# The opening of a transformer step: u's first products by one channel tile at a time, other queues for the small loads, weights asked for two chunks ahead

## The chip, the cores and the metric

The kernel runs on one core of a Trainium2 chip. It is one program, launched once. The metric is the device time of one execution in microseconds: 1690.18 in the median of three runs (1689.3 to 1690.31). The core has five engines with queues of their own: TensorE (PE, with its weight loads as PEld), VectorE (DVE), ScalarE (ACT), GpSimd (POOL) and SyncE (SP), which here only issues transfers.

## The reference, cut to what matters

One layer (D = 2048, 128 context tokens and 256 latent ones, so 384 token rows) does a token mixing and then an MLP. Only its beginning is touched by the change: the modulation's scale and shift, the normalised and modulated input h, and the first part of the projection h @ w_in.

```python
def _adaln(cond, ada_w, ada_b):
    mod = jax.nn.silu(cond) @ ada_w + ada_b
    return mod.reshape(cond.shape[0], N_MOD, D_MODEL)
...
    h = _rmsnorm(x, norm_w[0]) * (1 + scale_a) + shift_a
    proj = h @ w_in
    q, k, v, o, g, u = jnp.split(proj, [M, 2 * M, 3 * M, 4 * M, 4 * M + N_GATES * N_HEADS], axis=-1)
```

The context rows are modulated by c_ctx, the latent rows by c. u (1024 columns) feeds a pooling mixer, v and the gates g feed a bidirectional mLSTM; q, k, the output projection and the MLP come later.

## The kernel before

All products are in float32, split in two: an operand is a rounded part (hi) and the rest (lo), and a product takes three matmuls, hi by hi, lo of the input by hi of the weight, hi of the input by lo of the weight. ACT writes hi (L134 for weights, L447 for h), DVE writes lo (L135, L448). load_w loads a weight chunk through one of three raw buffers and splits it into one of N_W = 4 hi and 4 lo buffers.

The projection's u, v and gates are summed over the 16 channel tiles of 128 in eight steps of two tiles (ksteps). In each step h is formed for the two tiles by make_h, and five chunks of columns take their products (chunk list at L434): u 0 to 511, u 512 to 1023, and v in 384, 384 and 256 plus 32 gate columns. The sums of a chunk lie in three banks of the pool psum, one for each 128 token rows; the pool has eight banks of 128 x 512 floats, and everything that PE writes takes one of them. At a chunk's end the banks are copied to u_sb or vsb (first step, ACT, L514) or added there (later steps, DVE, L516).

h needs the scale (part 1 of ada_w) and the shift (part 0) of its channels. first_ada forms them for the two tiles of each step, as a generator that is advanced at places written out by hand: each next() issues a load of a slab of ada_w (512 KB: 128 partitions by 1024 floats) and its matmuls (L256), then copies the sum to SBUF (ada_sb, L268), and at last adds it up over the partition groups and finishes it (L272, ada_finish). For step 0 it goes matrix by matrix, four slabs of scale for both tiles, then four of shift, in buffers of the tags ada (four) and lo. For step 1 both go in one sum of eight slabs; from step 2 on ada_eight takes eight slabs at once (L365 and L372), some of them in the upper halves of u_sb and in masks, which are idle then.

x is loaded in three tiles (x_tok, tags x0 to x2 of the pool pre), squared and summed on ACT (L388), and transposed channel tile by channel tile on PE (transpose_x, L402), with a copy out of the bank on DVE for even and ACT for odd tiles. u_sb has the same three tags as x_tok, with one buffer each.

The order of PE, DVE and ACT up to order.close() (L478) is that of the program; X_ORDER spells it: t is a transpose, a advances first_ada, b forms the broadcast row of the norm (rbc). After L478 only PE's order is that of the program; the planner orders the others and SP by its costs. Before that, twelve of 16 tiles are transposed. After u's first chunk (XT_AT = 0) come the other four. ADA_STEPS says how often first_ada is advanced after each chunk of step 0; in later steps it is (1, 1, 1, 0, 0), and once more in the middle of chunk 3.

Chunk 0 of step 0 runs its three kinds of matmul one after the other, each over both tiles, so that lo may come later. Small loads (c_ctx, c, the first constants, and prm, which holds biases and norm weights) go out on ACT's queue (L79 to L91), x on SP's. In step 0 a chunk's split is queued behind the last instructions of make_h (h_ins).

Of the kernel before, what the change touches and what calls it, by code (L numbers as in the profile page):

```python
# [13 lines left out]
P = 128  # L14
# [11 lines left out]
N_CST = 15  # L26
# [4 lines left out]
XT_AT = 0  # L31
ADA_STEPS = (4, 0, 4, 0, 0)
X_ORDER = "tatatatattaatabata"
# [4 lines left out]
LAG = 4  # L38
RATES = (1.5, 1.3, 1.3)
# [4 lines left out]
def hymba_kernel(  # L44
# [6 lines left out]
    nc = tc.nc  # L51
# [27 lines left out]
    nc.scalar.dma_start(cc[:, 0, :], c_ctx.rearrange("(p j) -> p j", j=16))  # L79
    nc.scalar.dma_start(cc[:, 1, :], c[0].rearrange("(p j) -> p j", j=16))  # L80
    nc.scalar.dma_start(cst[:, 0:3], cs_src[:, 0:3])
# [6 lines left out]
    nc.scalar.dma_start(prm[0:96, 1, :], ada_b[0].rearrange("(r p) -> r p", p=P))  # L88
    nc.scalar.dma_start(prm[0:64, 0, :], norm_w[0].rearrange("i (k p) -> (i k) p", p=P))
    nc.scalar.dma_start(prm[64:72, 0, :], mlstm_norm_w[0].rearrange("(k p) -> k p", p=P))  # L90
    nc.scalar.dma_start(prm[72:80, 0, :], pool_scale[0].rearrange("(k p) -> k p", p=P))  # L91
# [252 lines left out]
    def first_ada():  # L344
        for k0, nk in ksteps:
            if k0 == 0:
                yield from ada_mat([(1, k0, nk)])
                yield from ada_mat([(0, k0, nk)], ("lo",))
            elif k0 == 2:
                yield from ada_mat([(0, k0, nk), (1, k0, nk)])  # L350
            else:
                yield from ada_eight(k0)
# [38 lines left out]
    xT = []  # L391
# [44 lines left out]
    def make_h(s, between=None):  # L436
        ts = []
        for k in range(ksteps[s][0], sum(ksteps[s])):
            t, hi, lo = slot(f"hm{k}"), slot(f"hh{k}", F32R), slot(f"hl{k}", F32R)
            ts.append((k, t, hi, lo))  # L440
            for g, (a, b) in enumerate(GROUPS):
                nc.vector.scalar_tensor_tensor(t[:, a:b], xT[k][:, a:b], mod[:, 1, k, g:g + 1], rbc[:, a:b], op0=ALU.mult, op1=ALU.mult)
# [22 lines left out]
    w_first = load_chunk(0, 0, later=lo_later)  # L465

    def shift_rows():
        for _ in range(2):
            transpose_x(len(xT), True)
        next(ada0)  # L470
        for _ in range(2):
            transpose_x(len(xT), True)

    h_ins = make_h(0, shift_rows)
# [5 lines left out]
    order2.enter_context(tc.manual_schedule(engines={mybir.EngineType.PE}))  # L480
    for s in range(NS):
        for ci, (kind, c0, w) in enumerate(chunks):
            k0, nk = ksteps[s]
            hi, lo, n = w_first if s == 0 and ci < 2 else load_chunk(s, ci, h_ins if s == 0 else ())
            if s == NS - 1 and ci == 4:
                with tc.issue_after(load_w.ins):
                    nc.sync.dma_start(masks, cs_src[:, 3:N_CST])
            acc = [bank(f"{kind}_{c0}_{s}_{i}") for i in range(3)]

            ways = ((0, 0), (1, 0), (0, 1))  # L490
            for ps in [ways[n:n + 1] for n in range(3)] if s == ci == 0 else [ways]:
                for k in range(nk):
                    for i in range(3):
                        for a, b in ps:
                            nc.tensor.matmul(acc[i][:, 0:n], h[k0 + k][a][:, i * P:(i + 1) * P], (hi, lo)[b][:, k, :],  # L495
                                             start=k == 0 and a + b == 0, stop=k == nk - 1 and b == 1)
                    if ci == 3 and k == 0:
                        next(ada0, None)
            if s == ci == 0:
                w_first = load_chunk(0, 1, h_ins)  # L500
# [5 lines left out]
            if ci == 3 and s < NS - 1:  # L506
                make_h(s + 1)
# [881 lines left out]
```

## Time and profile before

| | us |
|---|---|
| median of three runs | 1690.18 |
| lowest and highest | 1689.3 and 1690.31 |
| the profiled execution's own time | 1689.57 |
| its span, first to last instruction | 1687.9 |
| first product of u starts | 28.71 |

Times within the trace count from the span's start. The profiled execution lies 0.61 us under the median; 1.67 us of it lie outside the span. In a group of instructions of the timeline, the number after the start is the time from the first start to the last end; a bracket gives the idle time of the engine before it and what ended it. In the chain of waits each line is a piece of the path that ended last, with its start and length.

### The profile page before, as it was taken

What the parts mean: (1) busy time and instruction counts of PE and PEld (TensorE: products, weight loads), DVE (VectorE), ACT (ScalarE), POOL (GpSimd) and SP (SyncE); (2) the same over time, 40 slices, a digit from 0 to 9 for tenths busy, and PEclk for the clock granted to TensorE, in tenths of its full rate; (3) what the DMA queues carried; (4) which work ended last, traced back from release to release, by engine and by line L of the source; (5) the groups of instructions that cost most, each with busy time, mean ns of one, the idle gap of its engine ahead of it and who ended that gap; (6) DMA issues with size and microseconds to landing.
All of it is one profiled execution on the core that took longest, in us unless ns stands there. A gap on an engine that the chain in (4) does not pass through costs nothing.

```text
span 1687.9 us, 27859 instructions
## 1 busy us (share of the span) xinstructions
PE 1656.9 (98%) x10965; PEld 1582.5 (94%) x10965; DVE 1340.3 (79%) x2009; ACT 752.4 (45%) x1225; POOL 130.9 (8%) x181
## 2 busy tenths in 40 slices
PE   6999999999999999999999999999999999999997
PEld 4888999999999989989999999999999999999996
DVE  3677769898999959997797688988588488588688
ACT  4332355555443345543444444444444444444443
POOL 0000002221000024430000000000000000000120
PEclk9999999999999999999999999999999999999999
DMA  9999857777789964754546245544344443433653
GB/s 319 316 296 298 277 160 256 238 250 223 237 270 309 311 203 129 217 153 126 173 152 194 88 138 173 158 150 140 110 150 127 124 138 114 149 122 112 187 183 134
DMA packets 258195, 320.95 MB, mean 190 GB/s; under 512 B 14752, under 2 KB 223248, under 8 KB 257680
## 3 DMA queue, kind: packets, MB, share of 16 engines
q1 hardware_dynamic: 250256, 303.41, 57.0%
q0 software_dynamic: 5856, 13.69, 2.8%
q10 hardware_dynamic: 1952, 2.07, 0.4%
q8 instruction: 86, 1.41, 0.3%
q14 instruction: 45, 0.37, 0.1%
HBM read 308.61 MB, written 10.51 MB: 189 GB/s over the span
## 4 chain that ended last, share of the span: by engine, by line
PE 90%; DVE 4%; DMA 3%; issue 1%; SPq 1%; ACT 0%; POOL 0%; DVEq 0%; ACTq 0%; POOLq 0%
PE acc_w L144 10%; PE acc_w L143 10%; PE acc_w L145 10%; PE y L1223 4%; PE y L1224 4%; PE y L1222 4%; PE v L495 4%; PE u L495 3%; PE acc_wo L143 3%; PE acc_wo L144 3%; PE acc_wo L145 3%; PE y_yz L1223 2%; PE y_yz L1222 2%; PE y_yz L1224 2%; PE y L1066 2%; PE y L1065 2%
## 5 line engine op out<-in xcount | busy, mean ns | idle before, releaser
L144 PE MATMUL acc_w<-h2l,hi_w 128*128 128x384 f32 (+1 forms) x1024 | 346.2, 338 | 0.5 <-DVE h2l L1016 0.5
L143 PE MATMUL acc_w<-h2h,hi_w 128*128 128x384 f32 (+1 forms) x1024 | 344.2, 338 | 1.2 <-ACT h2h L1012 1.2
L145 PE MATMUL acc_w<-h2h,lo_w 128*128 128x384 f32 (+1 forms) x1024 | 345.1, 337 | 0.0
L135 DVE TENSOR_TENSOR lo_w<-raw_w,hi_w 128x1024 fp32r<-128x1024 f32 x152 | 185.3, 1221 | 137.0 <-ACT hi_w L134 136.8
L134 ACT ACTIVATE hi_w<-raw_w 128x1024 fp32r<-128x1024 f32 x152 | 160.8, 1058 | 215.2 <-PE acc_w L144 94.9
L316 DVE SCALAR_TENSOR_TENSOR ada_acc<-ada_raw,sg,ada_acc 128x1024 f32<-128x1024 f32 (+1 forms) x240 | 252.0, 1080 | 0.8 <-DMA ada_raw<-in_ada_w_dram 0.7
L143 PEld LDWEIGHTS acc_w<-h2h,hi_w 128*128 128x128 f32 x1024 | 192.2, 188 | 2.8 <-ACT h2h L1012 2.0
L144 PEld LDWEIGHTS acc_w<-h2l,hi_w 128*128 128x128 f32 x1024 | 192.6, 188 | 1.2 <-DVE h2l L1016 0.8
L145 PEld LDWEIGHTS acc_w<-h2h,lo_w 128*128 128x128 f32 x1024 | 192.4, 188 | 0.3 <-DVE lo_w L135 0.2
L1208 ACT ACTIVATE hi_t<-w 128x1024 fp32r<-128x1024 f32 x104 | 109.6, 1060 | 119.1 <-DVE w L1244 34.3
L1209 DVE TENSOR_TENSOR lo_t<-w,hi_t 128x1024 fp32r<-128x1024 f32 x104 | 126.3, 1220 | 15.1 <-ACT hi_t L1208 14.8
L1209 DVE TENSOR_TENSOR lo_b<-w,hi_b 128x1024 fp32r<-128x1024 f32 x78 | 95.3, 1221 | 41.9 <-ACT hi_b L1208 41.6
L1208 ACT ACTIVATE hi_b<-w 128x1024 fp32r<-128x1024 f32 x78 | 82.5, 1059 | 98.1 <-PE acc_w L144 66.7
L134 ACT ACTIVATE hi_wo<-raw_wo 128x1024 fp32r<-128x1024 f32 x32 | 34.0, 1064 | 80.6 <-DMA raw_wo<-in_w_out_dram 57.4
L942 ACT ACTIVATE z<-acc_w 128x384 f32<-128x384 f32 x54 | 26.3, 487 | 75.1 <-PE acc_w L145 75.1
L495 PE MATMUL v<-hi_v,hh 128*128 128x384 f32 (+1 forms) x144 | 48.0, 333 | 0.0
L134 ACT ACTIVATE hi_v<-raw_v 128x768 fp32r<-128x768 f32 (+1 forms) x24 | 19.0, 793 | 64.4 <-DMA raw_v<-in_w_in_dram 55.6
L495 PE MATMUL v<-lo_v,hh 128*128 128x384 f32 (+1 forms) x144 | 46.6, 324 | 1.0 <-DVE lo_v L135 1.0
L495 PE MATMUL v<-hi_v,hl 128*128 128x384 f32 (+1 forms) x144 | 46.5, 323 | 0.0
L135 DVE TENSOR_TENSOR lo_wo<-raw_wo,hi_wo 128x1024 fp32r<-128x1024 f32 x32 | 38.8, 1217 | 7.8 <-ACT hi_wo L134 7.0
L143 PE MATMUL acc_k<-hh,hi_k 128*128 128x384 f32 x128 | 44.2, 345 | 0.0
L143 PE MATMUL acc_o<-hh,hi_o 128*128 128x384 f32 x128 | 43.9, 343 | 0.0
(2264 smaller groups left out, 4549.0 us busy)
## 6 DMA issues: line engine op xcount, KB each, us to landing
raw_w<-in_w_dram SPq DMA_DIRECT2D x152, 512.0 KB, 4.2
ada_raw<-in_ada_w_dram SPq DMA_DIRECT2D x130, 512.0 KB, 4.7
w<-in_w_dram SPq DMA_DIRECT2D x104, 512.0 KB, 4.1
raw_wo<-in_w_out_dram SPq DMA_DIRECT2D x32, 512.0 KB, 5.1
u<-in_ada_w_dram SPq DMA_DIRECT2D x18, 512.0 KB, 6.6
raw_u<-in_w_in_dram SPq DMA_DIRECT2D x16, 512.0 KB, 7.0
raw_q<-in_w_in_dram SPq DMA_DIRECT2D x16, 512.0 KB, 4.8
raw_k<-in_w_in_dram SPq DMA_DIRECT2D x16, 512.0 KB, 4.9
```

Source lines behind the costliest of these rows:

```text
L134: nc.scalar.activation(hi[:, 0:n], raw[:, 0:n], AF.Copy)
L135: low = lambda: nc.vector.tensor_tensor(lo[:, 0:n], raw[:, 0:n], hi[:, 0:n].bitcast(F32), op=ALU.subtract)
L143: nc.tensor.matmul(ps, lh, rh, start=start, stop=False)
L144: nc.tensor.matmul(ps, lh, rl, start=False, stop=False)
L145: mm3.ins = nc.tensor.matmul(ps, ll, rh, start=False, stop=stop).ins
L316: nc.vector.scalar_tensor_tensor(acc[:, g, :], raw[:, a, :], cj, acc[:, g, :], op0=ALU.mult, op1=ALU.add)
L495: nc.tensor.matmul(acc[i][:, 0:n], h[k0 + k][a][:, i * P:(i + 1) * P], (hi, lo)[b][:, k, :], start=k == 0 and a + b == 0, stop=k == nk - 1 ...
L1208: nc.scalar.activation(hi, raw, AF.Copy)
L1209: nc.vector.tensor_tensor(lo, raw, hi.bitcast(F32), op=ALU.subtract)
L1222: nc.tensor.matmul(acc, xh, wh, start=start and j == 0, stop=False)
L1223: nc.tensor.matmul(acc, xh, wl, start=False, stop=False)
L1224: nc.tensor.matmul(acc, xl, wh, start=False, stop=stop and j == 3)
```

## The change

Step 0 is opened by one channel tile at a time. The scale and the shift of tile 0 are formed alone (slabs of 8 rows by 128 columns, still 512 KB, in place of 4 rows by 256), then those of tile 1. make_h takes a list of tiles and is called for tile 0 and for tile 1 in turn. chunk_mm is the old product loop; for u's two chunks in step 0 it is called first for tile 0 and later for tile 1, with the six sums (acc_first) kept open in between. PE's order there is now: u chunk 0 with tile 0, two slabs of tile 1's scale, u chunk 1 with tile 0, the end of that scale, a transpose, two slabs of the shift, the second make_h with two more transposes, then chunk 0 with tile 1.

Only six tiles of x are transposed in X_ORDER, two more in the first make_h; the last five (tiles 11 to 15) come after chunk 1 (XT_AT = 1). ADA_STEPS becomes (3, 2, 3, 0, 0).

load_ahead, called before each chunk's products, asks for the chunk itself and the two after it (N_AHEAD = 3) if they were not yet asked for. The loads of c_ctx, c and the constants move from ACT's queue to SP's, ahead of x; prm's four move from ACT's to POOL's.

```diff
--- before.py
+++ after.py
@@ -28,14 +28,15 @@
 N_W = 4
 N_ADA = 4
 N_E = 1
-XT_AT = 0
-ADA_STEPS = (4, 0, 4, 0, 0)
-X_ORDER = "tatatatattaatabata"
+XT_AT = 1
+ADA_STEPS = (3, 2, 3, 0, 0)
+X_ORDER = "ttatatabatta"
 N_X = 4
 RATE_GF = 0.4
 RATE_GS = 0.25
 S_FIRST, S_LAST, N_LAST = 1, 6, 2
 LAG = 4
+N_AHEAD = 3
 RATES = (1.5, 1.3, 1.3)
 GATE_AT = 1, 6, 10
 
@@ -76,19 +77,19 @@
     pre = pre_scope.enter_context(tc.tile_pool(name="pre", bufs=1))
     prm = pre.tile([P, 2, P], F32, name="prm")
     masks = vp.tile([P, N_CST - 3, P], F32, name="masks")
-    nc.scalar.dma_start(cc[:, 0, :], c_ctx.rearrange("(p j) -> p j", j=16))
-    nc.scalar.dma_start(cc[:, 1, :], c[0].rearrange("(p j) -> p j", j=16))
-    nc.scalar.dma_start(cst[:, 0:3], cs_src[:, 0:3])
+    nc.sync.dma_start(cc[:, 0, :], c_ctx.rearrange("(p j) -> p j", j=16))
+    nc.sync.dma_start(cc[:, 1, :], c[0].rearrange("(p j) -> p j", j=16))
+    nc.sync.dma_start(cst[:, 0:3], cs_src[:, 0:3])
 
     vsb = [vp.tile([P, NH, 129], F32, name=f"v{i}") for i in range(3)]
     gsb = vp.tile([P, 3, 32], F32, name="gsb")
     x_tok = [pre.tile([P, D], F32, tag=f"x{i}", name=f"xtok{i}") for i in range(3)]
     for t, src in zip(x_tok, (x_prompt[0], x_sample[0, 0:128], x_sample[0, 128:256])):
         nc.sync.dma_start(t, src)
-    nc.scalar.dma_start(prm[0:96, 1, :], ada_b[0].rearrange("(r p) -> r p", p=P))
-    nc.scalar.dma_start(prm[0:64, 0, :], norm_w[0].rearrange("i (k p) -> (i k) p", p=P))
-    nc.scalar.dma_start(prm[64:72, 0, :], mlstm_norm_w[0].rearrange("(k p) -> k p", p=P))
-    nc.scalar.dma_start(prm[72:80, 0, :], pool_scale[0].rearrange("(k p) -> k p", p=P))
+    nc.gpsimd.dma_start(prm[0:96, 1, :], ada_b[0].rearrange("(r p) -> r p", p=P))
+    nc.gpsimd.dma_start(prm[0:64, 0, :], norm_w[0].rearrange("i (k p) -> (i k) p", p=P))
+    nc.gpsimd.dma_start(prm[64:72, 0, :], mlstm_norm_w[0].rearrange("(k p) -> k p", p=P))
+    nc.gpsimd.dma_start(prm[72:80, 0, :], pool_scale[0].rearrange("(k p) -> k p", p=P))
     gbias = const.tile([P, 32], F32, name="gbias")
     nc.gpsimd.dma_start(gbias, gate_bias[0].rearrange("g h -> (g h)").partition_broadcast(P))
     mprev = const.tile([40, 3], F32, name="mprev")
@@ -344,8 +345,9 @@
     def first_ada():
         for k0, nk in ksteps:
             if k0 == 0:
-                yield from ada_mat([(1, k0, nk)])
-                yield from ada_mat([(0, k0, nk)], ("lo",))
+                for k in range(nk):
+                    yield from ada_mat([(1, k, 1)])
+                    yield from ada_mat([(0, k, 1)], ("lo",))
             elif k0 == 2:
                 yield from ada_mat([(0, k0, nk), (1, k0, nk)])
             else:
@@ -433,9 +435,9 @@
         nc.gpsimd.memset(vsb[i][:, :, 128:129], 1.0)
     chunks = [("u", 0, 512), ("u", 512, 512), ("v", 0, 3), ("v", 3, 3), ("v", 6, 2)]
 
-    def make_h(s, between=None):
+    def make_h(ks, between=None):
         ts = []
-        for k in range(ksteps[s][0], sum(ksteps[s])):
+        for k in ks:
             t, hi, lo = slot(f"hm{k}"), slot(f"hh{k}", F32R), slot(f"hl{k}", F32R)
             ts.append((k, t, hi, lo))
             for g, (a, b) in enumerate(GROUPS):
@@ -462,49 +464,72 @@
         return load_w(pieces, f"{kind}_{c0}_{s}", ksteps[s][1] * n, after, later) + (n,)
 
     lo_later = []
-    w_first = load_chunk(0, 0, later=lo_later)
-
-    def shift_rows():
-        for _ in range(2):
-            transpose_x(len(xT), True)
+    loaded = {0: load_chunk(0, 0, later=lo_later)}
+
+    def load_ahead(m, n):
+        for q in range(m, min(m + n, NS * len(chunks))):
+            if q not in loaded:
+                s, ci = divmod(q, len(chunks))
+                loaded[q] = load_chunk(s, ci, h_ins if s == 0 else ())
+                if q == NS * len(chunks) - 1:
+                    with tc.issue_after(load_w.ins):
+                        nc.sync.dma_start(masks, cs_src[:, 3:N_CST])
+
+    def shift_rows(before, behind, later):
+        for _ in range(before):
+            transpose_x(len(xT), later)
         next(ada0)
-        for _ in range(2):
-            transpose_x(len(xT), True)
-
-    h_ins = make_h(0, shift_rows)
+        for _ in range(behind):
+            transpose_x(len(xT), later)
+
+    def chunk_mm(acc, n, w, k0, ks, nk, by_way):
+
+        ways = ((0, 0), (1, 0), (0, 1))
+        for ps in [ways[m:m + 1] for m in range(3)] if by_way else [ways]:
+            for k in ks:
+                for i in range(3):
+                    for a, b in ps:
+                        nc.tensor.matmul(acc[i][:, 0:n], h[k0 + k][a][:, i * P:(i + 1) * P], w[b][:, k, :],
+                                         start=k == 0 and a + b == 0, stop=k == nk - 1 and b == 1)
+                yield
+
+    h_ins = make_h([0], lambda: shift_rows(1, 1, True))
     lo_later[0]()
     for copy in xt_late:
         copy()
     order.close()
     order2 = ExitStack()
     order2.enter_context(tc.manual_schedule(engines={mybir.EngineType.PE}))
+    load_ahead(1, 1)
+    acc_first = []
+    for ci in range(2):
+        kind, c0, w = chunks[ci]
+        acc_first.append([bank(f"{kind}_{c0}_0_{i}") for i in range(3)])
+        for _ in chunk_mm(acc_first[ci], w, loaded[ci], 0, [0], 2, True):
+            pass
+        if ci:
+            next(ada0)
+            transpose_x(len(xT))
+        for _ in range(2):
+            next(ada0)
+    h_ins = make_h([1], lambda: shift_rows(1, 1, False))
     for s in range(NS):
         for ci, (kind, c0, w) in enumerate(chunks):
             k0, nk = ksteps[s]
-            hi, lo, n = w_first if s == 0 and ci < 2 else load_chunk(s, ci, h_ins if s == 0 else ())
-            if s == NS - 1 and ci == 4:
-                with tc.issue_after(load_w.ins):
-                    nc.sync.dma_start(masks, cs_src[:, 3:N_CST])
-            acc = [bank(f"{kind}_{c0}_{s}_{i}") for i in range(3)]
-
-            ways = ((0, 0), (1, 0), (0, 1))
-            for ps in [ways[n:n + 1] for n in range(3)] if s == ci == 0 else [ways]:
-                for k in range(nk):
-                    for i in range(3):
-                        for a, b in ps:
-                            nc.tensor.matmul(acc[i][:, 0:n], h[k0 + k][a][:, i * P:(i + 1) * P], (hi, lo)[b][:, k, :],
-                                             start=k == 0 and a + b == 0, stop=k == nk - 1 and b == 1)
-                    if ci == 3 and k == 0:
-                        next(ada0, None)
-            if s == ci == 0:
-                w_first = load_chunk(0, 1, h_ins)
+            load_ahead(5 * s + ci, N_AHEAD)
+            hi, lo, n = loaded.pop(5 * s + ci)
+            early = s == 0 and ci < 2
+            acc = acc_first[ci] if early else [bank(f"{kind}_{c0}_{s}_{i}") for i in range(3)]
+            for k, _ in enumerate(chunk_mm(acc, n, (hi, lo), k0, [1] if early else range(nk), nk, early)):
+                if ci == 3 and k == 0:
+                    next(ada0, None)
             if s == 0 and ci == XT_AT:
                 while len(xT) < KT:
                     transpose_x(len(xT))
             for _ in range((ADA_STEPS if s == 0 else (1, 1, 1, 0, 0))[ci]):
                 next(ada0, None)
             if ci == 3 and s < NS - 1:
-                make_h(s + 1)
+                make_h(range(ksteps[s + 1][0], sum(ksteps[s + 1])))
             for i in range(3):
                 if kind == "u":
                     dst, src = u_sb[i][:, c0:c0 + w], acc[i][:, 0:n]
```

## The prediction, made before the changed kernel was timed

> **What bounds the kernel now.** First the page, for the shares, then busy time by stretches of the opening (columns: stretch, its length, busy us of PE, weight loads, DVE, ACT and POOL with instructions, granted clock, DMA share, GB/s).
>
> ```profile
> span 1687.9 us, 27859 instructions
> PE 1656.9 (98%) x10965; PEld 1582.5 (94%) x10965; DVE 1340.3 (79%) x2009; ACT 752.4 (45%) x1225; POOL 130.9 (8%) x181
> ```
>
> ```profile
> 0.00:28.70 28.70, 14.40 (x112) 7.28 (x112) 7.48 (x26) 12.42 (x23) 3.48 (x12) 1.00 0.96 318
> 28.70:46.00 17.30, 17.29 (x131) 12.86 (x131) 7.75 (x12) 10.11 (x19) 0.00 (x0) 1.00 1.01 327
> 46.00:65.60 19.60, 18.50 (x102) 15.65 (x102) 12.36 (x26) 9.17 (x17) 0.00 (x0) 1.00 0.96 311
> 65.60:87.00 21.40, 21.40 (x163) 17.90 (x166) 16.19 (x36) 6.52 (x11) 0.00 (x0) 1.00 0.91 298
> ```
>
> PE idles 31 us of the 1687.9, and 14.3 of them lie before 28.7. From there PE is the bound: 0.01 idle up to 46, 1.1 up to 65.6, nothing up to 87. DMA is at 0.96 to 1.01 of its time up to 65.6, so the opening is paced by loads. The chain of waits tells which.
>
> ```profile
> 18.73 8.55 DMA raw_u<-in_w_in_dram
> ...
> 27.31 1.06 ACT hi_u L134
> 28.37 0.30 ACT hh L447
> ...
> 28.71 4.63 PE u L495 x18
> 33.34 1.31 PE xt L402 x12
> 34.65 1.97 PE ada L256 x32
> 36.62 4.39 PE u L495 x18
> 41.01 3.16 PE v L495 x18
> 44.17 1.86 PE ada L256 x32
> 46.03 1.78 PE v L495 x9
> ...
> 65.61 3.59 PE ada L372 x64
> ...
> 86.95 3.59 PE ada L372 x64
> ```
>
> u's first product starts at 28.71, behind the last byte of x (3.15 MB), eight ada_w slabs (4.19 MB) and one weight chunk. Two later points are my marks: at 46.03 the last slab of the second pair (channel tiles 2 and 3) is multiplied, and at 65.61 begins the first block L372. From 65.61 to 86.95 a step takes 21.34 us of PE work without a wait, so whatever lead or lag the change has at 65.61 reaches the end unless a later wait gives or takes it.
>
> **The change, part by part.** *Small loads and x.* The seven small loads of ACT's queue and x's first load are eight transfers; the ninth, x's second load on SP, waited for the first.
>
> ```profile
> SPq L87 <- DMA cc<-in_c_ctx_dram: 4.8, 1, 4.8
> 13.90 0.47 PE L402 MATMUL xt<-cst,xtok 128*128 128x128 f32 x1 [2.10 <-DMA xtok<-in_x_sample_dram]
> DMA packets 236, 1.80 MB, mean 401 GB/s; under 512 B 16, under 2 KB 16, under 8 KB 16
> ```
>
> With prm on POOL's queue, the eight are cc twice, cst, x three times and two slabs, issued back to back. x's first load goes out about 1.35 us later (three issues of 0.45 ahead of it), its landing moves from 5.8 (0.8 plus 5.0, the transfer's time) to 7.1, and the two others follow at 1.05 MB / 401 GB/s = 2.6 each: all of x at 12.4 in place of 13.9. I take 1.5 us of gain; bounds nothing (the bytes are the same) and 4.8 (the whole wait). prm's four loads now go out on POOL, ahead of gbias, the state's stabilisers and its norm; the transposes that use prm stood at 7.42 and 8.28 and are needed only before x is there, the others later still.
>
> The Trainium skill, "Trainium Kernel Development and Optimization", section Key Constraints, says that loads issued from several engines run on the same 16 DMA engines and that spreading them saves only issue time. By that the new queues would gain nothing; the trace's 4.8 us row speaks against it. It is the fourth rival.
>
> *Slabs of one channel tile.* Eight loads of 512 KB remain, but rows of 512 bytes in place of 1024. Ten microseconds of 1 KB rows, and a short stretch at the kernel's end with rows of 512 bytes, give the price:
>
> ```profile
> q1 hardware_dynamic: 3551, 3.52, 109.7%
> q1 hardware_dynamic: 83, 0.04, 61.7%
> ```
>
> The first is 16 engines x 10 us x 1.097 / about 3440 data packets = 51 ns for 1024 bytes; the second 16 x 0.2 x 0.617 / about 69 = 28 ns for 512. A slab takes 3.52 MB per 10 us = 1.5 us before; with 28/25.5 of it 1.65, and I take 1.7 (bounds 1.5 and 1.8, the latter without overlap of packets). "DMA: Bandwidth & Descriptors", Specifications, of the Trainium skill puts line rate at 512 bytes and up, which would make it 1.5; the rows show about a tenth more.
>
> Loads needed for u's start: two slabs for the scale, two for the shift, one chunk: 12.4 + 4 x 1.7 + 1.4 = 20.6. Then hi_u 1.06, hh 0.34 and gaps: **u starts at 22.5, 6.2 earlier.** Lower bound 21.8; upper 24.5, if PE's small work behind x (six transposes, slabs, rbc, rows) queues.
>
> *From there to the second mark*, PE's order is written out, so I add. Nine products are half of 4.39, 2.2. A slab of 8 instructions of 256 columns took 1.97/4 = 0.5; of 128 columns there are 16 instructions, each between half as long and as long, so 0.5 to 1.0: I take 0.7. The tail from the last slab product to the first product is copied from
>
> ```profile
> 26.76 0.38 ACT L268 ACTIVATE ada_sb<-ada 128x256 f32<-128x256 f32 x1 [0.17 <-PE ada L256]
> 27.91 0.16 DVE L280 TENSOR_TENSOR mod<-ada,prmT 128x4 f32<-128x4 f32 x1 [0.85 <-PE ada L272]
> 30.19 1.22 DVE L135 TENSOR_TENSOR lo_u<-raw_u,hi_u 128x1024 fp32r<-128x1024 f32 x1
> ```
>
> from 26.76 to 28.07, plus hh's 0.30: 1.6. It was paid once before u; now it is paid again in the middle for the second tile, with nothing else in PE's order but two transposes. Before, its like was hidden by loads. u's first lo comes 1.22 behind hl: 0.4 of waiting.
>
> Start 22.5; u chunk 0, tile 0: 2.2 + 0.4 = 25.1; two slabs 26.5; chunk 1, tile 0: 28.7; rows and a transpose 29.2; two slabs 30.6; tail 32.2; chunk 0, tile 1: 34.4; three slabs 35.9; chunk 1, tile 1: 38.1; five transposes; two slabs 1.0; v 3.16; three slabs 1.5. The loads stay ahead: 20.6, then u 1.4, four slabs 6.8, v 1.1, three slabs 4.5 give 34.4 for the third of them. The eighth slab's buffer is the fourth's, free only at 43.8, so it lands some 4 later: 48, just in time for the slab's turn at 48.5 (row below); the next step's loads (two u, eight slabs, three v, 18 us of DMA) then end near 65.
>
> ```profile
> raw_w<-in_w_dram SPq DMA_DIRECT2D x152, 512.0 KB, 4.2
> ```
>
> *The five transposes* (tiles 11 to 15) are where I choose.
>
> ```profile
> 22.44 0.55 PE L402 MATMUL xt<-cst,xtok 128*128 128x128 f32 x3
> 23.03 0.56 DVE L410 COPY xT<-xt 128x384 f32<-128x384 f32 x1 [0.62 <-PE xt L402]
> 34.03 0.49 ACT L408 ACTIVATE xT<-xt 128x384 f32<-128x384 f32 x1 [2.58 <-PE xt L402]
> 34.46 0.60 ACT L514 ACTIVATE u<-u 128x512 f32<-128x512 f32 x1
> ```
>
> u's sums were done at 33.34, ACT was idle, and yet u's copy out came at 34.46, when x's last transpose was through: u's buffer is x's (the tags x0 to x2). So with the transposes behind chunk 1, the three banks of chunk 0 and the three of chunk 1 stay held; one more holds the open ada sum. Of eight, one is left, and each transpose waits for the copy of the one before, and PE, which is in order, holds the slabs and v behind it: 0.55 + 0.56 (or 0.49) + two hand-overs of 0.04 = 1.15. Five take 0.55 + 4 x 1.15 = 5.2. Before, with free banks, twelve instructions took 1.31, five tiles would take 1.65. Bounds 1.65 and 5.2 plus four conversions (rivals).
>
> 38.1 + 5.2 + 1.0 + 3.16 + 1.5 = 49.0 against 46.03: **3.0 late** at the first mark, though u started 6.2 early. What ate it: second tail 1.6, transposes 3.6, twice as many ada instructions, and work that PE did before 28.7 in its loads' shadow.
>
> *Weights ahead.* load_ahead asks for chunks two further on, ahead of the slabs on SP. Waits that this should end:
>
> ```profile
> 62.55 0.45 PE L495 MATMUL v<-lo_v,hh 128*128 128x384 f32 x1 [1.02 <-DVE lo_v L135]
> 108.54 4.40 DMA raw_u<-in_w_in_dram
> 114.10 0.28 ACT ada_sb L268
> 100.00:120.00 20.00, 19.16 (x149) 15.82 (x148) 14.41 (x29) 6.37 (x10) 0.42 (x1) 1.00 0.93 291
> ```
>
> Of the 1.1 idle up to 65.6, this wait is 1.02 and a conversion of u's fourth chunk the rest; the 0.84 in 100 to 120 is ada's copy on ACT behind a late raw_u. Together 1.94; bounds 0 and 1.94, and I take 1.9, since weights come earlier and PE later. What the loads ahead wait for: a raw buffer (three), free when chunk q-3 is converted, and a hi and a lo (four), free when the products of q-4 are done; both lie far back. If this cover fails, the weights ahead cost what the third rival says. The masks' load, the renamed make_h and chunk_mm issue what was issued before: nothing.
>
> **Sum:** +3.0 - 1.9 = +1.1 us. The profiled execution took 1689.57 (span 1687.9 and 1.67 around it), 0.61 under the median 1690.18. So 1690.7 for such an execution, and 1691.3 as a median.
>
> **Rivals.**
> 1. *No chain of transposes*: a bank comes free earlier, or loads are late enough to hide it. Five tiles take 1.65: 3.55 less, 1687.7; with halved slab instructions at 0.5 (six on the path: 1.2 less) and the earliest start, about 1685.8. For it: bank limits do not show before. Against: u's late copy out.
> 2. *Conversions inside the chain*, the slower one. ACT and DVE are free to take a hi (1.06) or lo (1.22) between two copies. Place: tiles 11 to 15. Price: four links at 1.06 to 1.22, some 4.5, 1695.8. It decides as soon as a chunk lands while the chain runs, with its conversion set ahead of the copy; v's third chunk and the next step's u are due there. Against: ACT is busy only 10.1 of 17.3 us.
> 3. *Weights ahead delay the slabs* in the six L372 steps: DMA runs at 0.91 to 0.96, and two v chunks (about 2 us) now go ahead of the last slabs. At 0.8 each, 4.8: 1696.1. Against: a step has 21.34 us for some 18 of loads.
> 4. *The opening hardly moves*: x lands at 13.9 as before, u starts at 24.0: 1.5 more, 1692.8.
>
> **How the numbers follow.** Forecast 0.46, rival 1 0.20, rival 2 0.14, rival 3 0.08, rival 4 0.12. A measurement tells apart about 0.2%, 3.4 us: below 1686.8 is faster, above 1693.6 slower. Faster takes most of rival 1's lower part and little of the forecast: 0.16. Slower is rivals 2 and 3: 0.22 and a tail of 4, less what is mild of them: 0.22. Same 0.62. The range leaves a tenth on each side: 1686.2 to 1695.6.
>
> **What would show it.** u's first product at 22 to 23; a second wait for hh at about 31; transposes 11 to 15 about 1.1 apart, each behind a copy, and u's copy out only after the last; no wait on lo_v near 62; the first L372 block at 66 to 67. I am wrong if that block starts before 64 or after 69, if the transposes run back to back, or if L372 blocks lie more than 21.5 apart.

## The result, and the profile after

| | before | after |
|---|---|---|
| median, 13 executions each on the same chips (us) | 1689.27 | 1692.80 |
| lowest and highest | 1686.05 and 1690.55 | 1690.25 and 1694.16 |
| profiled execution, its span | 1689.57, 1687.9 | 1693.88, 1692.1 |
| first product of u starts | 28.71 | 27.77 |
| second mark (last slab of the second pair multiplied) | 46.03 | 54.42 |
| first block of eight slabs | 65.61 | 72.12 |

The ratio is 1.0022, 95% interval [1.0014, 1.003]: the change costs about 3.7 us. That lies inside the forecast range; the point, +1.1 us, was too low. The stretches of the kernel after, in the columns of the prediction's table, cut at the same times:

```profile
0.00:28.70 28.70, 13.47 (x99) 8.34 (x100) 7.14 (x25) 12.54 (x23) 5.57 (x16) 1.00 0.99 293
28.70:46.00 17.30, 15.60 (x143) 10.39 (x143) 7.96 (x15) 4.66 (x10) 0.00 (x0) 1.00 0.88 260
46.00:65.60 19.60, 18.37 (x130) 15.14 (x129) 10.24 (x23) 13.05 (x27) 0.00 (x0) 1.00 0.98 327
```

Between 28.7 and 46, PE was busy 17.29 of 17.30 us and DMA at 1.01 before. Now PE idles 1.7 us there and DMA is at 0.88: neither is full, so the stretch has become a chain of waits. The first 28.7 us moved less per second than before (293 GB/s in place of 318). The chain of waits names the pieces (start, length, what; ada L257 are slab products, xt transposes, bc_rx the norm's row):

```profile
16.41 1.08 PE ada L257 x16
17.49 0.83 PE xt L404 x3
18.32 1.01 PE ada L257 x16
19.34 0.83 PE xt L404 x3
20.17 0.23 PE ada L273 x2
...
21.31 1.65 PE bc_rx L209 x2
22.95 1.01 PE ada L257 x16
...
34.19 0.39 PE xt L404 x3
34.58 1.01 PE ada L257 x32
...
37.23 2.72 PE u L492 x9
...
43.65 0.34 PE xt L404 x3
44.02 0.50 ACT xT L410
44.56 0.56 PE xt L404 x3
45.14 0.57 DVE xT L412
...
48.08 0.55 PE xt L404 x3
48.63 1.00 PE ada L257 x16
...
54.42 1.78 PE v L492 x9
...
72.12 3.59 PE ada L374 x64
...
93.46 3.59 PE ada L374 x64
```

Three things are to be seen. First, the same work has two prices. 16 slab products take 1.01 us at 22.95, and 32 take 1.01 at 34.58; three transposes take 0.83 at 17.49 and 0.39 at 34.19. Up to some 25 us PE works at half its later pace. The granted clock of 1.00 in the first row does not speak against that: the column is made from the trace's clock entries (start, length, granted share), a stretch counts as full where there is none, and in this kernel the first entry begins at 25.55 us, where the pace doubles. Kernels in which the clock falls later, inside the entries, show the slow pace as a granted clock of 0.50 (gbias_late and warm below). Second, from 43.65 on the five transposes alternate with their copies, as forecast, until slabs and v follow at 48.63. Third, from 54.42 the kernel takes 17.70 us to its first block, where before took 19.58.

The forecast put u's start at 22.5; it came at 27.77. x landed last at 14.5, not 12.4, and the page of DMA queues for the stretch from 7 to 10 us shows a suspect (queue: packets, MB, share of 16 engines):

```profile
q1 hardware_dynamic: 89, 0.72, 62.2%
q0 software_dynamic: 87, 0.02, 39.8%
```

POOL's queue (q0) moves 0.02 MB but holds 39.8% of the 16 DMA engines' time: 16 x 3 us x 0.398 = 19 us for 87 packets. One of the transfers on it is the gate bias, 128 bytes copied to each of 128 partitions.

### The profile page after: what moved, and what is told of

Its sections match the earlier page's. It is cut to its first block, busy times and chain, and to the rows that moved or that the text cites. A ratio compares the mean times of both kernels' runs of the same rounds, so it can differ in the third digit from the quotient of the medians.

```text
span 1692.1 us, 28004 instructions
## 1 busy us (share of the span) xinstructions
PE 1660.1 (98%) x11029; PEld 1585.4 (94%) x11029; DVE 1341.2 (79%) x2012; ACT 750.7 (44%) x1227; POOL 133.2 (8%) x185
## 4 chain that ended last, share of the span: by engine, by line
PE 88%; DVE 6%; DMA 3%; issue 2%; ACT 1%; POOL 0%; SPq 0%; DVEq 0%; ACTq 0%; POOLq 0%
PE acc_w L146 10%; PE acc_w L145 10%; PE acc_w L144 10%; PE v L492 4%; PE u L492 4%; PE y L1248 4%; PE y L1249 4%; PE y L1247 4%; PE acc_wo L144 2%; PE acc_wo L146 2%; PE acc_wo L145 2%; PE y_yz L1247 2%; PE y_yz L1248 2%; PE y_yz L1249 2%; PE y L1091 2%
## 5 line engine op out<-in xcount | busy, mean ns | idle before, releaser
L144 PE MATMUL acc_q<-hh,hi_q 128*128 128x384 f32 x128 | 43.9, 343 | 0.0
```

The source lines that it names most:

```text
L144: nc.tensor.matmul(ps, lh, rh, start=start, stop=False)
```

## The experiments

Each ratio is to the kernel before on the same chips, with its 95% interval. Marks within a kernel come from its one profiled execution. First the change taken apart without the split opening.

**Queues alone.** Kernel before; only the small loads move, as in the change.

```diff
-    nc.scalar.dma_start(cc[:, 0, :], c_ctx.rearrange("(p j) -> p j", j=16))
+    nc.sync.dma_start(cc[:, 0, :], c_ctx.rearrange("(p j) -> p j", j=16))
...
-    nc.scalar.dma_start(prm[0:96, 1, :], ada_b[0].rearrange("(r p) -> r p", p=P))
+    nc.gpsimd.dma_start(prm[0:96, 1, :], ada_b[0].rearrange("(r p) -> r p", p=P))
...
```

> The kernel before with only the small loads moved (c_ctx, c and constants to SP ahead of x, prm to POOL). In the changed kernel x landed at 14.5 instead of 13.9, although it was issued 3 us earlier; between 8 and 10 the packets of the broadcast gate bias on POOL's queue took 1.4 to 2.1 us each and x's few. Theory A: the move gains nothing, u's start at 28.7 to 29.5, total 0 to +0.8 against the kernel before. Rival (the prediction's step, x at 12.4): u's start at 27.2, total 1.5 under the kernel before.

Measured: 1.0001 [0.9992, 1.001], 1689.98 us beside 1688.74. x lands at 15.0, u starts at 30.5, the first block at 67.2: in the opening the moved loads lose 1.7 us, more than theory A allowed, of which the total shows nothing certain (the profiled execution, 1692.54, was the slowest of the twelve). x is 1.1 later than before, and the half pace lasts longer too: the first clock entry begins at 22.0, in the kernel before at 18.9. That the queues would bring x 1.5 us earlier was wrong as the change stands.

**Weights ahead alone.** Kernel before with load_ahead (N_AHEAD = 3).

```diff
...
-            hi, lo, n = w_first if s == 0 and ci < 2 else load_chunk(s, ci, h_ins if s == 0 else ())
+            load_ahead(5 * s + ci, N_AHEAD)
+            hi, lo, n = loaded.pop(5 * s + ci)
...
```

> The kernel before with the weights asked for two chunks ahead, and nothing else of the change. Theory A (the weights ahead end the waits of 1.0 to 1.9 us before the first L372 block and of 1.1 near 113, and cost nothing): total 2 to 3 us under the kernel before. Rival: the order of loads only pushes the slabs back and PE waits for them in the L372 steps: same or up to 3 above the kernel before.

Measured: 0.9994 [0.9986, 1.0003], 1688.55 beside 1688.74. The chain of waits of this kernel, from the second mark on:

```profile
46.97 1.78 PE v L503 x9
...
49.30 1.23 DVE lo_u L136
...
51.10 1.14 DVE hm L443 x3
...
53.70 8.36 PE u L503 x35
...
65.20 3.59 PE ada L373 x64
```

The wait on lo_v near 62 is gone. But the loads ahead make a slab late (PE waits for it up to 36.9), so that the second mark comes at 46.97, 0.9 later than before, and the stretch from the second mark to the block takes 18.23 us (19.58 before, 17.70 after): conversions of weights that now come early stand on DVE around hm and ahead of hl, and u's products wait for hl until 53.70. In the timeline, which puts a block's start 0.07 us ahead of the chain's, the blocks start at 65.13, 86.47, 107.75 and 129.01, where before has 65.54, 86.89, 108.16 and 130.52: 0.4 earlier at the first, and the wait near 113 gave its 1.1 us. The total is the same within its interval: the gains of theory A are there but small, and the late slab is what the rival named, though not in the L373 steps.

**Queues and weights**: the whole change except the split.

> The change without the split: the small loads moved and the weights two chunks ahead, the opening by pairs of tiles and its transposes as before. Theory A (the split of the opening, with its late transposes, costs the changed kernel some 3.5 to 4.5): u's first product at 30 to 30.5 as with the moved loads alone, total 1688.5 to 1689.5, within 0.8 of the kernel before and 3 to 4.5 under the changed one. Rival (the moved loads cost most): total 1691 or more.

Measured: 0.999 [0.9981, 0.9999], 1686.95 beside 1688.13. u starts at 30.0 and the first block at 65.7, much as before. So the sign of the whole change is the split's: 0.999 without it, 1.0022 with it, and the intervals are apart.

**The same, with the gate bias's load late**, behind POOL's norm.

```diff
-    nc.gpsimd.dma_start(gbias, gate_bias[0].rearrange("g h -> (g h)").partition_broadcast(P))
...
     rstd_cols(rx, ss, 3, 1.0 / D)
+    with tc.issue_after(rstd_cols.ins):
+        nc.gpsimd.dma_start(gbias, gate_bias[0].rearrange("g h -> (g h)").partition_broadcast(P))
```

> The kernel before, its opening not split, with the small loads moved, the gate bias late and the weights two chunks ahead. Theory A (loads set that opening, so x earlier moves everything, and the weights ahead end two later waits): x at 12.9, u's first product near 27.7 instead of 28.7, total 2 to 3 under the kernel before. Rival (u's start hangs on the eight slabs, not on x): u at 28.5, total as the weights ahead alone, 0.2 to 1 under the kernel before.

Measured: 0.9987 [0.9978, 0.9996], 1686.23 beside 1689.05. It is the fastest kernel here and beats the kernels before and after, by little; against the run before it, the gate bias's place makes no difference that the intervals could show. The total came as theory A expected, but not by its path: x lands at 13.1, 0.8 earlier than in the kernel before, and u starts at 29.1, 0.4 later, with the half pace lasting to 21.25 in place of 18.9. The first block, at 64.5, owes its lead to the weights: from the second mark it takes 18.3 us in place of 19.6.

Now the split, with its suspects taken away one at a time.

**After, with the gate bias late** (the same edit).

> The changed kernel with the gate bias's broadcast load queued on POOL behind the norm's power instruction, at about 18 us, instead of beside x. Theory A (the broadcast load is what holds x up between 8 and 10): the third x tile is there at 12.9 to 13.2 instead of 14.5, u's first product 0.7 to 1.3 earlier than 27.8, total 0.7 to 1.3 under the changed kernel. Rival (x is slow because its loads start behind cc and the constants): x at 14.3 or later, no difference in the total.

Measured: 1.0023 [1.0013, 1.0033], 1692.88 beside 1689.05. The queues from 7 to 10 us:

```profile
q1 hardware_dynamic: 174, 1.27, 100.6%
q0 software_dynamic: 140, 0.01, 3.6%
```

The main queue moves 1.27 MB in place of 0.72, and x lands at 12.7, close to the forecast's 12.4. That settles most of x: the gate bias, which in the kernel after ran beside x's transfer, cost it 1.8 us. u starts at 26.4, 1.4 earlier, yet the total is the same. PE's timeline shows where it went (start, length from first start to last end, count at the end, idle before it in brackets):

```profile
12.70 1.11 PE L405 MATMUL xt<-cst,xtok 128*128 128x128 f32 x4 [1.99 <-DMA xtok<-in_x_sample_dram]
...
46.69 0.90 PE L405 MATMUL xt<-cst,xtok 128*128 128x128 f32 x3 [0.65 <-DVE xT L413]
47.52 1.94 PE L256 MATMUL ada<-ada_raw,cT 128*32 128x256 f32 x16
```

At the end of the chain of transposes PE falls to half pace: 16 slab products take 1.94 where the kernel after takes 1.00 in its chain at 48.63, and v's products lie 0.32 apart until 53, where they lie 0.18 afterwards. The granted clock (third column from the end) shows it, here first and in the kernel after second:

```profile
46.30:53.00 6.70, 6.31 (x30) 4.72 (x31) 2.22 (x3) 4.36 (x8) 0.00 (x0) 0.50 0.71 245
46.30:53.00 6.70, 5.47 (x45) 4.22 (x48) 1.38 (x3) 5.62 (x11) 0.00 (x0) 1.00 0.83 288
```

The first block comes at 73.5, later than in the kernel after. This run and the one before it differ by the split alone: the medians, 1692.88 and 1686.23 on the same chips, lie 6.6 us apart, the two profiled executions 9.1, of which 9.0 are there at the first block. The fall in pace is 2.8 of those: from the last transpose's start to the second mark (55.81) take 9.1 us, in the kernel after 6.3 (48.08 to 54.35 in the timeline). Whether the other executions had this fall is not recorded.

**After, with five transposes early**, right behind chunk 0 of tile 0, while banks are free.

```diff
+        else:
+            for _ in range(5):
+                transpose_x(len(xT))
```

> The changed kernel with five more transposes of x right behind u's chunk 0 with tile 0, where five banks are free, so that none is left behind chunk 1. Theory A (PE's written order sets the opening; one free bank made five transposes 5.1 us long instead of 1.7): transposes back to back, the first L372-type block about 3.4 us earlier than the 72.1 of the changed kernel, total 3.4 under the changed kernel, about 1689.4 when that has 1692.8. Rival L (the slabs of ada_w set the pace, the transposes fill time that PE would wait for loads anyway): PE waits for slabs instead, total within 0.8 of the changed kernel.

Measured: 1.0014 [1.0005, 1.0024], 1692.01 beside 1688.74.

```profile
30.57 1.80 PE L404 MATMUL xt<-cst,xtok 128*128 128x128 f32 x15
...
53.00 0.64 PE L257 MATMUL ada<-ada_raw,cT 128*32 128x256 f32 x8 [0.85 <-DMA ada_raw<-in_ada_w_dram]
```

All fifteen now run in 1.80 us, with no copy between them, so the chain of banks was real: v's first chunk starts at 47.0 in place of 49.6. But the second mark comes only 0.8 earlier, and the total is within the 0.8 us of the rival. PE meets slabs that are not there, and SP's waits up to 60 us say why (total, times, longest):

```profile
SPq L253 <- PE ada L257: 13.5, 4, 7.5
```

A slab can be loaded only when one of four buffers is free, and these come free as PE gets to them. Behind the chain of banks stood a chain of buffers.

**The same with six slab buffers.** They fit only with 50 in place of 55 of the small tiles (slots). Eight buffers with 45 small tiles (t_ring) gave no time: that program deadlocks.

```diff
-N_ADA = 4
+N_ADA = 6
-N_SLOT = 55
+N_SLOT = 50
```

> The five transposes early, as in t_early, with six buffers for ada_w's slabs in place of four (and 50 in place of 55 of the small slots, to make room). In t_early the transposes ran back to back and yet v's first chunk and the slabs behind it ended only 0.8 earlier than in the changed kernel, because PE now waited for the last three slabs of the second pair, whose loads SP had held back until PE freed a buffer (longest wait 7.5). Theory A (four slab buffers that PE frees late): the second chunk of v starts by 51 instead of 53.6, the first L372-type block at 68.5 to 69.5 instead of 71.3, total 2 under t_early, about 1690. Rival L (the transfers themselves are too slow): v's second chunk still at 53, total as t_early.

Measured: 1.0047 [1.0034, 1.0061], 1696.69 beside 1688.13. v's first chunk to the second mark takes 4.78 us in place of t_early's 6.53: the waits for slabs are gone. But x came at 15.7 here, and PE ran at half pace from 42.4 to 45.8. With the gate bias late besides:

> The split opening with what was found in its way taken away: transposes early, six slab buffers (50 small slots), the gate bias late. Theory A (no chain of transposes and no held-back slabs, but PE still at half pace until about 25 and the second tile's tail in the middle): u at 26.4, first L372-type block at 66.5 to 68, total 1688 to 1689.5, still above the unsplit kernel with the same loads (1686.2). Rival (the split pays once nothing is in its way): that block at 64 or earlier, total under 1686.2.

Measured: 1.0028 [1.0017, 1.0039], 1693.22 beside 1688.13. u starts at 27.9, not 26.4: x lands at 15.0 here, although the gate bias is late. Its first tile landed at 9.6, in gbias_late at 7.6; why, stays open. The second mark is at 51.85 and the first block at 69.57, the best of the split kernels but behind both expectations, and still 5.0 behind the unsplit one with the same loads (64.53).

Those two totals carry the smaller pool too. **Kernel before with N_SLOT = 50 alone:**

> The kernel before with N_SLOT 50 in place of 55, nothing else. It prices the smaller pool that the runs with six slab buffers had. Theory (their later stages lost to fewer slots): first L372 block at 65.5 as before, and in all 1.5 to 3 us more than before. Rival (the pool's size costs nothing and their loss is the split's): within 0.5 us of before.

Measured: 1.0053 [1.0041, 1.0066], 1698.39 beside 1688.63. The first block is where it was (65.43), and the loss comes later. Five small tiles fewer cost some 9 us, more than the theory's 1.5 to 3, so the totals of the two kernels above say nothing against the split; only their marks in the opening do. split_free is 4.1 us behind this kernel at the first block and 2.3 at q's first product (202.59 and 200.27), and yet its ratio is the lower one. Whether the split with six buffers and 55 slots would pay can't be said; it does not fit.

**Warm PE.** The kernel after with six matmuls on constants while PE waits for x (each shows as two records); nobody reads their sums.

> The changed kernel with six matmuls on constants added on PE between the transposes of prm and the first transpose of x; nobody reads their result. In the changed kernel PE takes twice the later time for the same instruction until about 25 (slab of 16 instructions 1.01 against 0.51, three transposes 0.83 against 0.34). Theory A (PE works slowly because it idled before, and this delays u): slabs from 16 on take 0.5, u's first product starts near 25 instead of 27.8, total 2 to 3 under the changed kernel. Rival L (loads of x, four slabs and one chunk set u's start): u's start moves by under 0.7 us, since the chunk lands at 23.0 and its split and h take 1.5 anyway; total within 1 us of the changed kernel.

Measured: 1.0025 [1.0017, 1.0034], 1692.96 beside 1688.74.

```profile
8.98 5.43 PE L387 MATMUL warm<-cst 128*128 128x384 f32 x12
...
16.63 0.64 PE L257 MATMUL ada<-ada_raw,cT 128*32 128x128 f32 x16 [1.24 <-DMA ada_raw<-in_ada_w_dram]
...
18.35 0.96 PE L257 MATMUL ada<-ada_raw,cT 128*32 128x128 f32 x16 [0.60 <-DMA ada_raw<-in_ada_w_dram]
```

The first slab is fast (0.64 in place of 1.08), the second is not any more: PE waited 1.24 us ahead of the first and 0.60 ahead of the second. u starts at 27.7, as in the kernel after. The granted clock, by stretches:

```profile
11.80:18.50 6.70, 4.75 (x41) 2.77 (x43) 1.25 (x4) 4.98 (x9) 0.88 (x1) 1.00 1.13 326
18.60:25.30 6.70, 5.78 (x45) 3.52 (x37) 1.84 (x6) 0.77 (x2) 0.00 (x0) 0.50 1.14 329
```

So the pace follows what PE did shortly before, and six matmuls don't last until u: the run can't tell theory A from the rival. One more run therefore also fills the waits behind them:

```diff
-    for op in X_ORDER:
+    for n_op, op in enumerate(X_ORDER):
+        if op != "t" and 0 < n_op:
+            for _ in range(2 if n_op == 2 else 1):
+                nc.tensor.matmul(warm[:, 0:NTOK], ident, cst.rearrange("p n q -> p (n q)"), start=True, stop=True)
```

> The kernel after, with matmuls on constants whose sums nobody reads: six ahead of x and one or two more ahead of each slab and of the norm's row in the opening, where PE waits for loads. Theory (PE's slow pace before u, in which three transposes take 0.83 us in place of 0.39 and a slab 1.08 in place of 0.5, costs u's start some 2.5 us, and short waits bring it back): the slabs ahead of u take 0.5 to 0.64 us each, the norm's row 0.8, u starts at 25 to 26, and the second mark comes 0 to 2 us earlier (53 to 54.4), since slabs pace what follows; in all 1690.5 to 1692.8 beside 1692.8. Rival (the loads alone pace u's start; PE's pace there is covered): u starts at 27.2 to 28.2 as in the kernel after, though the steps are short.

Measured: 1.0051 [1.0036, 1.0066], 1699.15 beside 1688.63; u starts at 27.08.

```profile
21.23 0.91 PE L209 MATMUL bc_rx<-dg_rx,cst 128*128 128x384 f32 x2 [0.16 <-DVE dg_rx L207]
21.98 0.81 PE L426 MATMUL warm<-cst 128*128 128x384 f32 x2
22.71 0.64 PE L257 MATMUL ada<-ada_raw,cT 128*32 128x128 f32 x16
...
24.00 0.81 PE L426 MATMUL warm<-cst 128*128 128x384 f32 x2
24.74 0.64 PE L257 MATMUL ada<-ada_raw,cT 128*32 128x128 f32 x16
...
27.08 1.13 PE L499 MATMUL u<-hi_u,hh 128*128 128x512 f32 x3 [0.46 <-ACT hh L456]
```

Every step is at full pace, but from the norm's row on PE no longer waits for loads, and the two fillers at 21.98 and 24.00 stand on the path themselves, 0.73 and 0.74 us. From the row to u it takes 5.85, less the fillers 4.38; the kernel after takes 6.46 (21.31 to 27.77). So the slow pace costs u about 2.1 us there. That subtraction is an estimate; the next run has the pace without the fillers. And u's 0.7 us did not reach the end: PE was slow again from 36.5 to 43.4 and from 50.2 to 57.0 (granted clock 0.50), around new waits, and the first block came at 78.1, 6.0 behind the kernel after. That is about the loss in the total (6.35 between the two medians, some 4.9 by the ratios), and neither expectation foresaw it.

**After with N_AHEAD = 1**, that is, each chunk asked for when it is due.

> The changed kernel with each chunk's weights asked for only when its turn comes (N_AHEAD = 1). Theory A (the weights ahead gave back about 1.9 before the first L372-type block and 1.1 near 113 of what the opening lost): that block 1 to 2 later than 72.1, total 1.5 to 3 over the changed kernel. Rival (PE came later anyway, so the waits would have gone without it): within 0.8 of the changed kernel.

Measured: 1.0053 [1.004, 1.0067], 1696.48 beside 1689.05; without the weights ahead the kernel loses 0.3% more. Its profiled execution (1692.7) was the fastest of its five, so the trace shows only part of it: PE at half pace behind the chain (16 slab products in 1.94), the first block at 72.9, and the third 21.7 us behind the second, where the kernel after takes 21.3. From its second mark (55.27) to the first block it takes 17.70 us, just as the kernel after does. So up to there the rival is right: the waits are gone without the weights ahead, because PE comes late. Of the 0.3% this trace shows 0.45 us, at the third block; the rest was not traced.

This trace also has what warm_all lacked. Up to u PE's order is that of the kernel after, but here the clock came back at 20.4, ahead of the norm's row:

```profile
21.77 0.91 PE L209 MATMUL bc_rx<-dg_rx,cst 128*128 128x384 f32 x2 [0.92 <-DVE dg_rx L207]
22.61 0.64 PE L257 MATMUL ada<-ada_raw,cT 128*32 128x128 f32 x16
...
26.32 1.13 PE L492 MATMUL u<-hi_u,hh 128*128 128x512 f32 x3 [0.47 <-ACT hh L449]
```

From the row to u it takes 4.55 us without a filler, the kernel after 6.46. x landed 0.7 later (15.2) than there, and yet u starts 1.45 earlier. So the slow pace costs u 1.9 us behind the row, here by a measurement; the 2.1 above was close.

## Why the prediction was right in its range and wrong in a step

| step | forecast | measured in the kernel after |
|---|---|---|
| last x tile used | 12.4 | 14.5 (12.7 in gbias_late) |
| u starts | 22.5 | 27.8 |
| from u's start to the second mark | 26.5 | 26.6 |
| second mark against before | +3.0 | +8.4 |
| taken back by 136 us (in the forecast, by the weights ahead) | 1.9 | 3.0 |
| span against before | +1.1 | +4.2 |

*Right: the chain of transposes.* One free bank, each transpose behind the copy before it. The forecast had 1.15 a link; the starts 44.56 and 48.08 are three links apart, 1.17 each, and u's copy out comes only after the last:

```profile
44.02 0.49 ACT L410 ACTIVATE xT<-xt 128x384 f32<-128x384 f32 x1 [4.25 <-PE xt L404]
...
48.45 1.58 ACT L539 ACTIVATE u<-u 128x512 f32<-128x512 f32 x3 [1.04 <-PE xt L404]
```

t_early shows that banks were the cause: with free ones the link vanishes. Rival 1 (no chain) and rival 2 (conversions inside it) both fall; ACT took one conversion at 46.7, behind a copy, and delayed none. The second tail in the middle, 1.6, is there too, from the end of the slabs at 35.59 to u's product at 37.23.

*Right: the rest between u's start and the second mark*, 26.6 for 26.5, in part by luck, since its terms were off and cancelled. 16 slab products of 128 columns take 0.5 at full pace, not 0.7, which is 0.8 less over the four slabs; against that, the nine u products at 37.23 took 2.72 in place of 2.2, and the first nine, with their wait for lo, 3.0 in place of 2.6.

*Wrong: the size of u's start, the step "12.4 + 4 x 1.7 + 1.4, then hi_u and hh".* It is 5.3 us off, and all of the miss at the second mark is this one term (8.4 against 3.0). Its parts: x, 2.1, of which the gate bias is 1.8 (gbias_late); slabs of 512-byte rows, which by the transfers' records landed 1.80 us apart in place of 1.7 (1.50 in the kernel before), 0.4 in all; and 2.8 in PE's small work, which the forecast took at the pace of later stages. The queue of PE's small work stood in it as the upper bound, 24.5, sized too low. Of the 2.8, 1.9 is the half pace from the norm's row to u (no_ahead). Ahead of the row the second slab, its transposes and the sum of the scale, 1.01, 0.83 and 0.23 in the chain, ran slow as well; in warm_all's chain they take 0.57, 0.48 and 0.13. By estimate that is 0.9 more, and with it the 2.8 is whole. In the kernel before, the same slow steps lay in the shadow of the loads. By pulling u forward, the change took the loads out of the way and made PE's slow opening the path.

*Right in number, not in cause: the weights ahead.* The stretch from the second mark to the first block fell by 1.9, as forecast in all. But no_ahead takes the same 17.70 us there: the fall is due to PE's lateness, and the agreement is luck. The wait near 113 gave another 1.1; there w_alone, with the weights ahead and an early PE, gave 1.1 as well, while no_ahead lost only 0.45 up to 136 us. From there to the end a further 1.2 came back; by which waits was not traced. So 4.2 of the 8.4 us at the second mark came back, where the forecast had 1.9 and another cause, and that the time lies so near the forecast is luck to that extent.

*Rival 3* (weights ahead hold up the slabs) falls: L374 blocks lie 21.3 apart. *Rival 4* gave 1692.8, just what was measured, but not by its path: x was worse than unmoved, u 3.8 us later than it had, and more came back behind it. The Trainium skill, "Trainium Kernel Development and Optimization", section Key Constraints, says that more queues save only issue time. Without the collision x lands at 13.1 (before_best) and 12.7 (gbias_late) beside 13.9, 0.8 and 1.2 earlier, and not 1.5, but at 15.0 in split_free; whether what was gained is issue time alone, no run shows.

Is the split wrong in itself? With the gate bias, the chain of banks and the chain of buffers all taken away (split_free), u starts 1.3 us earlier than in the unsplit kernel (before_best, 29.13). But from u's start to the first block it takes 41.7 us; the unsplit kernel takes 35.4. The two stretches, split first:

```profile
27.85:69.57 41.72, 40.33 (x304) 31.92 (x305) 22.86 (x45) 19.40 (x39) 0.00 (x0) 1.00 1.03 328
29.13:64.53 35.40, 35.09 (x225) 28.78 (x225) 21.44 (x40) 18.77 (x37) 0.00 (x0) 1.00 1.04 335
```

The clock is full in both. Of the 6.3 us, 5.2 are work of PE (mainly slab products, transposes and sums that used to be done before u, in the loads' shadow) and 1.1 are waits. So the split gains 1.3 us at u and pays 6.3 behind it, most of it in work, as the forecast had it in kind.

## What to carry to other kernels

Starting a stage earlier pays only if the work it overtakes was waiting, not if that work merely ran for nothing beside a load. Before moving an engine's work out of such a shadow, price it at the pace that the trace shows there, not at that of a busy stage. Read that pace from what the same instruction takes, or from the granted clock of a stretch of a few us; a long stretch averages it away. Where each buffer pool is full, expect one chain behind another: here free banks led straight to waits for slab buffers, and the room for more of those came from a pool whose cut alone cost 0.5%.

## What the runs showed of the hardware

PE has a slow pace of half speed, and it is the granted clock: three transposes take 0.83 or 0.39 us, 16 slab products of 256 columns 1.94 or 1.00, and stretches with the higher figure show 0.50 wherever the trace has clock entries (gbias_late, warm). Before a trace's first entry the column says 1.00 whatever the pace.

Where the clock fell again in the opening, it stayed at half for 3.41 us (no_ahead, t_ring6) or 6.83 (gbias_late, warm, twice in warm_all), and the entries' lengths are multiples of 3.41. Counted in such steps from the first entry, the clock fell after steps in which PE was busy 1.5 to 1.7 us (gbias_late 1.64, from 42.80 to 46.21, with waits of 0.58 to 0.65 us). In the kernel after, the same chain of transposes fell into two steps (42.62 to 46.03 and on to 49.44) with 2.18 us each, and the pace held. That reads as if a step's share of work decided, and as if the chain cost more or less by where the steps happen to lie. It is a reading of six falls, not a test, and one does not fit: t_ring6 lost its clock after a step with 2.25 us.

The Trainium skill, "TensorE: Matmul & The Clock Gate", section "A second HAM failure mode: psum-queue depth-cycling", tells of short idle times between groups of matmuls, from cycling through banks, that drop the clock to half again and again. The traces agree: behind the chain of banks gbias_late, no_ahead and warm_all have a granted clock of 0.50 for 3.4 to 6.8 us.

Later in the span such stretches come and go as well: the kernel before has one of 3.41 us at 544.6, w_alone and before_best have none there. By estimate one costs half its length, 1.7 us, so single executions differ by that much for reasons that lie outside the opening.

A load that copies 128 bytes to 128 partitions took engine time out of all proportion to its bytes (39.8% of 16 engines for 0.02 MB; 3.6% for 0.01 MB without it) and cost x 1.8 us. And five small tiles fewer, in a kernel whose first block they didn't touch, cost 0.53%.
